# Layer 1's feed-forward with seven products of sums of half blocks in place of eight

## The chip, the core and the metric

The kernel runs on one core of one Trainium2 chip. The metric is the device time of one execution in microseconds, and less is better. The core's engines work from queues of their own: TensorE (PE in the profile, with its weight loads as PEld) multiplies, VectorE (DVE), ScalarE (ACT) and GpSimd (POOL) do the elementwise work, and SyncE (SP) issues nearly all of the transfers (DMA) between SBUF and DRAM. Products are accumulated in eight PSUM banks.

## The reference, cut to what matters

A two-layer transformer trunk works on 1024 tokens of width 1024, with 256 context tokens in layer 0. Each layer has a mixer and a gated feed-forward with 2816 hidden features. Layer 1's feed-forward and the final norm are what the change touches:

```
def _swiglu(x, w_in, w_out):
    a, b = jnp.split(x @ w_in, 2, axis=-1)
    return (jax.nn.silu(a) * b) @ w_out

x = x + mx[5] * _swiglu(_modulate(_rms(x, norm_ffn[layer]), mx[3], mx[4]),
                        ffn_in[layer], ffn_out[layer])
...
return _rms(x, norm_final)
```

Everything is float32. The kernel gets near float32 with reduced-precision products: each operand is split into a high part and a low part, and a product is three matmuls (high by high, low by high, high by low; `mm3`, L104 to 107).

## The kernel before, in words

**Layout.** Features lie on the 128 partitions. The 1024 tokens are two chunks of 512 (`c` = 0 and 1). A tile of activations is [128, 8, 512]: eight blocks of 128 features. `act` holds four buffers of 16 KB per partition (tag a16) and two of 8 KB (a8).

**A pair of parts.** `split` (L94 to 102) makes them: ACT copies the source to the high part (L96), DVE (L100) or POOL (L102) subtracts it for the low part. `load_w` (L240 to 252) loads a weight block [128, 1024] on SP's queue into `raw` and splits it. It takes pools pwA and pwB in turn.

**Layer 1's mixer output.** `MixerOut.block` (L786 to 795) multiplies one of eight weight blocks with one chunk, adds the result to the residual `x[c]` on DVE (L793) and adds its square to a running sum (`Rms.add`, ACT L187/L190 and POOL L194). Chunk 0 is finished inside the retention stage, chunk 1 in the `sweep`. `Rms.finish` (L196 to 213) sums over partitions with PE (L203), takes the power -1/2 with Ln and Exp on ACT (L208, L209), corrects it (L210, L211) and leaves the scale vector `rstd` (L213). `Rms.apply` (L215 to 224) multiplies (L218, DVE) and splits (L223 ACT, L224 DVE). The normalization of a chunk is deferred: it is put into the queues behind the first product of the next work (`run_deferred`).

**The feed-forward, `ffn` (L815 to 857).** The hidden features are 22 blocks (`j`, NJ). For each block and chunk, `f_in` makes two products over eight k-blocks (24 matmuls each), ACT takes Silu of the first (L827), DVE multiplies by the second (L828), and the result is split into `hh` and `hl`. `f_out` multiplies it with eight column blocks of the output weights (24 matmuls) and adds each to `x[c]` with the gate (L845, DVE). `f_out` runs one step behind `f_in`. The hidden result stays in SBUF, and every output product is added to the residual at once.

**The end.** In `final1` (L1402) chunk 1's last output runs in two halves of 256 tokens, and `done1` defers each part's final norm and stores (L1395, L1397).

**What sets the order.** The program text is handed to a planner, which gives each engine its queue: among the instructions whose inputs and buffers are there it takes the one that comes first in the text. On the chip each queue is then worked off in that order. Memory pools are a stack: a pool opened after others were closed lies on their bytes, its tags one after the other in the order of first use. With `reuse_waits="tile"` a new tile waits for the users of the earlier tiles on its own bytes, and for nothing else. Before layer 1's feed-forward the stack, above `act`, is pwA (20 KB: raw 4, wh 8, wl 8), `x[0]` (16), the small tiles t2j (20), `x[1]` (16) and pwB3 (24).

Of the kernel before, what the change touches and what calls it, by code (L numbers as in the profile page):

```python
# [39 lines left out]
def dit(ctx, tc, A, out):  # L40
# [50 lines left out]
    def col(name, n):  # L91
        return cols[:, CO[name] : CO[name] + n]
# [10 lines left out]

    def mm3(ps, wh, wl, xh, xl, first, last):  # L104
        te.matmul(ps, wh, xh, start=first, stop=False)  # L105
        te.matmul(ps, wl, xh, start=False, stop=False)  # L106
        te.matmul(ps, wh, xl, start=False, stop=last)  # L107
# [24 lines left out]
    def ada_block(l, typ, b, whichs):  # L132
        blk = typ * KB + b
        if (l, typ) not in parts:
            parts[l, typ] = T(cst, [P, KB, 2, 2], f"pt_{l}{typ}")
        for h in range(2):
            w = T(cst, [P, 512], "adaw", bufs=2)
            with tc.issue_after(mark[0]):
                sy.dma_start(w, A["ada"][l, blk, h])
            for which in whichs:  # L140
                jk = T(cst, [P, 1024], "junk", BF16)
# [132 lines left out]

# [1 line left out]
    ocd = [T(dram, [P, 8, n], f"oc{c}") for c, (_, n) in enumerate(CH)]  # L276
# [182 lines left out]
    def v_post(gi):  # L459
# [5 lines left out]
        for i, tb in enumerate(tbs):  # L465
# [37 lines left out]

# [1 line left out]
    sD = es()  # L505
# [93 lines left out]

# [1 line left out]
    sE = es()  # L601
# [147 lines left out]
    sA.close()  # L749
# [1 line left out]
    psE = es()  # L751
# [213 lines left out]
    sL2.close()  # L965
# [1 line left out]
    SC = 64 ** -0.5  # L967
# [26 lines left out]

# [1 line left out]
    psI = es()  # L996
# [155 lines left out]
    sG.close()  # L1152
# [1 line left out]
    psJ = es()  # L1154
# [209 lines left out]
    sJ.close()  # L1364
# [24 lines left out]
    def done1(c, s):
        def later(r=rm1[c]):  # L1390
            n = r.n
            r.finish()
            for b in range(KB):
                y = x[c][:, b, s]
                ve.scalar_tensor_tensor(y, y, col("nfin", 8)[:, b : b + 1], r.r[:, :n], op0=ALU.mult, op1=ALU.mult)  # L1395
                if b % 2:
                    sy.dma_start(out[c, :, b - 1 : b + 1, s], x[c][:, b - 1 : b + 1, s])  # L1397

        run_deferred()
        deferred.append(later)  # L1400

    def final1(f_in, f_out, prev):  # L1402
        f_in(NJ - 1, 0)
        prev()
        f_in(NJ - 1, 1)
        f_out(NJ - 1, 0)
        f_out(NJ - 1, 1, slice(0, 256))
# [117 lines left out]
```

## Time and profile before

| | |
|---|---|
| median of 3 runs | 2883.57 us (2882.09 to 2884.86) |
| span of the profiled execution | 2883.5 us |
| mean granted TensorE clock | 0.982 |
| q1, SP's transfers | 210.89 MB |
| layer 1's mixer output and feed-forward | from about 2080 us to the end |

The profile is one execution. Its page gives busy times and shares of each engine, the span in 40 slices, the chain of work that ended last, and groups of instructions with their count, busy time, mean ns of one, and the idle time ahead of them with what ended it. A view of the trace answers for a stretch of time: a row of the timeline is start, duration, engine, line, operation, output<-inputs and shape; a row of the windows is, for a stretch, the busy time and count of each engine, the granted clock, the share of the transfer engines and GB/s. Matmuls overlap, so the duration of one (0.39 us) is longer than the distance between two.

### The profile page before, as it was taken

How to read it: one execution, taken by the hardware profiler on the slowest of the kernel's cores; microseconds unless marked ns; L12 is line 12 of the kernel's file. 1: busy time of each engine (PE TensorE's matmuls, PEld its weight loads, DVE VectorE, ACT ScalarE, POOL GpSimd, SP SyncE). 2: the span in 40 equal slices, each digit the busy share in tenths (PEclk: the TensorE clock that was granted, in tenths of full speed). 3: DMA queues.
4: the chain of work that ended last, by engine and by line, in shares of the span. 5: the costliest groups of instructions: out<-in, count | busy, mean ns of one | idle time of the engine just before them, and what ended most of it. 6: DMA issues, size and time to landing. Idle time of an engine off the chain costs nothing.

```text
span 2883.5 us, 35705 instructions
## 1 busy us (share of the span) xinstructions
PE 2740.1 (95%) x13928; PEld 2308.7 (80%) x13928; DVE 1716.4 (60%) x3174; ACT 931.5 (32%) x1579; POOL 769.1 (27%) x476
## 2 busy tenths in 40 slices
PE   6998899998999999999999899898899999999997
PEld 4876788787888888888888787786688888888886
DVE  8779776457665555564445546887654444444446
ACT  5425455544111111111113434676551111111113
POOL 2132122352111212121213146443342112211222
PEclk8999999999999999999999999999999999999998
DMA  6343010441222222221111122124321111111111
GB/s 234 106 149 105 25 37 27 169 131 63 70 70 74 81 66 73 66 88 45 44 37 62 70 92 78 63 63 135 123 74 59 44 44 51 52 51 44 44 44 59
DMA packets 90649, 217.37 MB, mean 75 GB/s; under 512 B 8816, under 2 KB 24944, under 8 KB 89456
## 3 DMA queue, kind: packets, MB, share of 16 engines
q1 hardware_dynamic: 88800, 210.89, 22.5%
q8 instruction: 110, 1.80, 0.3%
q0 software_dynamic: 432, 2.62, 0.2%
q10 hardware_dynamic: 1248, 1.57, 0.1%
q14 instruction: 59, 0.48, 0.1%
HBM read 193.03 MB, written 22.02 MB: 75 GB/s over the span
## 4 chain that ended last, share of the span: by engine, by line
PE 71%; DVE 14%; DMA 5%; ACT 4%; issue 3%; POOL 2%; SPq 0%; POOLq 0%; DVEq 0%; ACTq 0%
PE ps L105 22%; PE ps L107 22%; PE ps L106 22%; DVE junk L142 3%; DMA adaw<-in_ada_dram 3%; PE ps L686 1%; DVE t2k L218 1%; DVE sm L1083 1%; DVE st L666 1%; ACT P L669 1%; DVE spt L100 1%; PE ps L183 1%; POOL wl L102 1%; ACT wh L96 1%; PE ps L203 1%
## 5 line engine op out<-in xcount | busy, mean ns | idle before, releaser
L105 PE MATMUL ps<-a,wh 128*128 128x512 f32 (+1 forms) x2488 | 929.2, 374 | 15.7 <-ACT a L223 7.1
L106 PE MATMUL ps<-a,wl 128*128 128x512 f32 (+1 forms) x2488 | 921.7, 371 | 10.1 <-DVE wl L100 7.6
L107 PE MATMUL ps<-a,wh 128*128 128x512 f32 (+1 forms) x2488 | 919.9, 370 | 2.5 <-DVE a L224 1.8
L102 POOL TENSOR_TENSOR wl<-raw,wh 128x1024 fp32r<-128x1024 f32 x181 | 445.8, 2466 | 1400.0 <-ACT wh L96 1399.7
L105 PEld LDWEIGHTS ps<-a,wh 128*128 128x128 f32 x2488 | 474.1, 191 | 101.1 <-ACT a L223 9.1
L106 PEld LDWEIGHTS ps<-a,wl 128*128 128x128 f32 x2488 | 473.6, 190 | 94.4 <-DVE wl L100 10.4
L107 PEld LDWEIGHTS ps<-a,wh 128*128 128x128 f32 x2488 | 473.4, 190 | 82.9 <-DVE a L224 3.6
L828 DVE TENSOR_TENSOR t2k<-t2k,ps 128x512 f32<-128x512 f32 (+1 forms) x110 | 69.6, 633 | 624.6 <-PE ps L107 624.6
L105 PE MATMUL ps<-hh,wh 128*128 128x512 f32 (+1 forms) x888 | 327.2, 368 | 4.1 <-ACT hh L96 2.5
L107 PE MATMUL ps<-hl,wh 128*128 128x512 f32 (+1 forms) x888 | 325.8, 367 | 1.1 <-DVE hl L100 1.1
L106 PE MATMUL ps<-hh,wl 128*128 128x512 f32 (+1 forms) x888 | 326.3, 367 | 0.0
L845 DVE SCALAR_TENSOR_TENSOR x<-ps,md,x 128x512 f32<-128x512 f32 (+1 forms) x528 | 312.3, 653 | 4.6 <-PE ps L107 4.6
L96 ACT ACTIVATE wh<-raw 128x1024 fp32r<-128x1024 f32 x193 | 203.9, 1058 | 276.8 <-PE ps L107 157.9
L827 ACT ACTIVATE t2k<-ps 128x512 f32<-128x512 f32 (+1 forms) x110 | 61.1, 555 | 672.0 <-PE ps L107 671.9
L845 DVE SCALAR_TENSOR_TENSOR xk<-ps,md,xk 128x512 f32<-128x512 f32 (+1 forms) x360 | 241.0, 730 | 3.2 <-PE ps L107 3.2
L142 DVE CUSTOM_DVE_ANT_0 junk<-adaw,cond_x 128x512 bf16<-128x512 f32 x160 | 132.2, 826 | 172.4 <-DMA adaw<-in_ada_dram 170.3
L96 ACT ACTIVATE hh<-t2k 128x512 fp32r<-128x512 f32 (+1 forms) x110 | 64.2, 584 | 410.7 <-DVE t2k L828 410.7
L105 PEld LDWEIGHTS ps<-hh,wh 128*128 128x128 f32 x888 | 168.2, 189 | 33.1 <-ACT hh L96 2.9
L107 PEld LDWEIGHTS ps<-hl,wh 128*128 128x128 f32 x888 | 167.9, 189 | 29.0 <-DVE hl L100 1.5
L106 PEld LDWEIGHTS ps<-hh,wl 128*128 128x128 f32 x888 | 168.1, 189 | 27.4 <-issue 0.2
L100 DVE TENSOR_TENSOR hl<-t2k,hh 128x512 fp32r<-128x512 f32 (+1 forms) x110 | 135.0, 1228 | 2.9 <-ACT hh L96 1.8
L194 POOL TENSOR_TENSOR acc<-t2k,acc 128x512 f32<-128x512 f32 (+1 forms) x71 | 84.5, 1192 | 134.9 <-ACT t2k L190 132.7
(277 smaller groups left out, 3565.8 us busy)
## 6 DMA issues: line engine op xcount, KB each, us to landing
raw<-in_w_fi_dram SPq DMA_DIRECT2D x88, 512.0 KB, 3.7
adaw<-in_ada_dram SPq DMA_DIRECT2D x160, 256.0 KB, 2.7
raw<-in_w_fo_dram SPq DMA_DIRECT2D x44, 512.0 KB, 3.7
raw<-in_w_cd_dram SPq DMA_DIRECT2D x26, 512.0 KB, 3.7
raw<-in_w_cdo_dram SPq DMA_DIRECT2D x16, 512.0 KB, 3.8
raw<-in_w_abo_dram SPq DMA_DIRECT2D x14, 512.0 KB, 3.8
a<-in_ada_dram SPq DMA_DIRECT2D x12, 512.0 KB, 9.7
t2k<-oc SPq DMA_DIRECT2D x24, 256.0 KB, 3.1
```

Of the source, the lines that this page charges most:

```text
L96: ac.activation(hi, src, AF.Identity)
L100: ve.tensor_tensor(lo, src, f32(hi), op=ALU.subtract)
L102: po.tensor_tensor(lo, src, f32(hi), op=ALU.subtract)
L105: te.matmul(ps, wh, xh, start=first, stop=False)
L106: te.matmul(ps, wl, xh, start=False, stop=False)
L107: te.matmul(ps, wh, xl, start=False, stop=last)
L142: ve.tensor_tensor_reduce(jk[:, :512], w, cond[which][:, h * 512 : h * 512 + 512], op0=ALU.mult, op1=ALU.add, scale=1.0, scalar=0.0, accum ...
L183: te.matmul(self.ps, ones, sq[:, :n], start=self.count == 1, stop=self.count == self.total)
L194: po.tensor_tensor(self.acc[:, :n], sq[:, :n], self.acc[:, :n], op=ALU.add)
L827: ac.activation(s[:, :n], pa, AF.Silu)
L828: ve.tensor_tensor(s[:, :n], s[:, :n], pb, op=ALU.mult)
L845: ve.scalar_tensor_tensor(xm, ps[:, s], mod(l, which(c), GATE_F, m), xm, op0=ALU.mult, op1=ALU.add)
```

## The change

With A the weights and B the activations, a product of 2 x 2 half blocks is made from seven products instead of eight (Winograd's form of Strassen's method). For the input half, A is the block's two halves a and b by two halves of the features, and B is two halves of the features by two chunks. The sums of B (T1 to T4) are made once; the sums of A (S1 to S4, `comb_w`) for every block.

- `Seven.first` (chunk 0 alone) makes B11 and B21; `Seven.second` makes B22 and T1 to T4 from both chunks, in place in `x[0]` and `x[1]`. The residual is therefore stored to DRAM before (`spill`, `xr`) and read back later.
- `fin_front(j)` makes the two products A11 B11 and A12 B21 of a block with weights of its own (`fr`, `w1`), up to LEAD = 3 blocks ahead; `fin_back(j)` loads the block's weights again, makes the sums, and the other five products, with three read-outs between products that share a bank.
- The hidden result of two blocks gives the seven B operands of the output half (`hid_out`), which go to DRAM (`hd`); the sums of the output weights go to DRAM too (`wo_out`, `sd`).
- The output half (`fout`) runs one of the seven products at a time over all of the hidden features, in 6 steps each; `load_b` reads both operands of a step from DRAM and splits them, two steps ahead in the text. Two groups of four banks hold the sums, and x is updated only at the end of each product. Chunk 0's final norm comes before the seventh product.
- Pools: pA, opened when the pools of the mixer and x are closed, holds fr (8 KB), w1 (16), acc (6), g0 (8), w8 (48) and t2k (16), in this order; pT, with T1 and T4, lies at the other end of the memory. To make room, the tiles of the condition (cond_x, adaw, junk) move to a pool at that end that is closed after layer 0, POOL's transfer scratch is cut to 1024 bytes, and the three stores of `oc` go from POOL's queue to SP's.

```diff
-        po.dma_start(ocd[c][:, 4:8], u[c])
+        sy.dma_start(ocd[c][:, 4:8], u[c])
...
+        def first(self, r):
+            self.scaled(0, r)
+            self.plain("B11", 0, 0)
+            self.plain("B21", 0, 1)
+
+        def second(self, r):
+            x0, x1 = self.x
+            self.scaled(1, r)
+            lo4, hi4 = slice(0, 4), slice(4, 8)
+            ve.tensor_tensor(x0[:, lo4], x1[:, lo4], x0[:, lo4], op=ALU.subtract)
+            for k in range(4):
+                ve.scalar_tensor_tensor(x1[:, k], x1[:, k + 4], self.d[k], x1[:, k], op0=ALU.add, op1=ALU.subtract)
+            self.plain("B22", 1, 1)
+            for k in range(4):
+                y = x1[:, k + 4]
+                ve.scalar_tensor_tensor(y, y, self.sh[k + 4], x0[:, k], op0=ALU.add, op1=ALU.subtract)
+            self.comb("T2", x1[:, hi4], "dve")
+            self.comb("T3", x1[:, lo4], "pool")
+            for k in range(4):
+                y = x0[:, k + 4]
+                ve.scalar_tensor_tensor(y, y, self.sh[k + 4], x1[:, k + 4], op0=ALU.add, op1=ALU.subtract)
+            self.comb("T1", x0[:, lo4], "dve")
+            self.comb("T4", x0[:, hi4], "pool")
+
+    def comb_w(raw, e):
+
+        e.tensor_tensor(raw[:, 3], raw[:, 2], raw[:, 3], op=ALU.add)
+        e.tensor_tensor(raw[:, 2], raw[:, 0], raw[:, 2], op=ALU.subtract)
+        e.tensor_tensor(raw[:, 0], raw[:, 3], raw[:, 0], op=ALU.subtract)
+        e.tensor_tensor(raw[:, 1], raw[:, 1], raw[:, 0], op=ALU.subtract)
...
+    def fin_front(l, j):
+        raw = T(pA, [P, 2, 512], "fr", F32, 2)
+        sy.dma_start(raw.rearrange("p a n -> p (a n)"), A["w_fi"][l, j, 0])
+        w = T(pA, [P, 2, 2, 512], "w1", F32R, 2)
+        w = w[:, 0], w[:, 1]
+        cut(w[0], w[1], raw, "pool")
+        X = T(pp, [P, 512], "ps")
+        mm4(X, w, 0, "B11", True, True)
+        s1 = t2k("acc")
+        ac.activation(s1, X, AF.Identity)
+        Y = T(pp, [P, 512], "ps")
+        mm4(Y, w, 1, "B21", True, True)
+        g = T(pA, [P, 512], "g0", F32, 4)
+        ve.tensor_tensor(g, Y, s1, op=ALU.add)
+        ac.activation(g, g, AF.Silu)
+        pre[j] = X, g
+
+    def fin_back(l, j):
+        X, g0 = pre.pop(j)
+        raw = w8([P, 4, 512])
+        for h in range(2):
+            sy.dma_start(raw[:, 2 * h : 2 * h + 2].rearrange("p a n -> p (a n)"), A["w_fi"][l, j, h])
+        w2 = w8([P, 2, 1, 512], F32R)
+        cut(w2[:, 0], w2[:, 1], raw[:, 3:4], "dve")
+        comb_w(raw, ve)
+        w3 = w8([P, 2, 2, 512], F32R)
+        cut(w3[:, 0], w3[:, 1], raw[:, 0:2], "pool")
+        w4 = w8([P, 2, 2, 512], F32R)
+        cut(w4[:, 0], w4[:, 1], raw[:, 2:4], "dve")
+        w2, w3, w4 = ((w[:, 0], w[:, 1]) for w in (w2, w3, w4))
+        mm4(X, w3, 0, "T2", False, True)
+        u1 = t2k("acc")
+        ac.activation(u1, X, AF.Identity)
+        Z = T(pp, [P, 512], "ps")
+        mm4(Z, w4, 0, "T3", True, True)
+        m7 = t2k("acc")
+        ac.activation(m7, Z, AF.Identity)
+        mm4(X, w4, 1, "T1", False, True)
+        h1 = t2k()
+        ve.tensor_tensor(h1, X, m7, op=ALU.add)
+        mm4(Z, w2, 0, "T4", False, True)
+        h0 = t2k()
+        ve.tensor_tensor(h0, Z, u1, op=ALU.add)
+        mm4(X, w3, 1, "B22", False, True)
+        g1 = T(pA, [P, 512], "g0", F32, 4)
+        ac.activation(g1, X, AF.Silu)
+        ve.tensor_tensor(h0, h0, g0, op=ALU.mult)
+        ve.tensor_tensor(h1, h1, g1, op=ALU.mult)
+        hid[j] = h0, h1
...
+    for j in range(LEAD):
+        fin_front(1, j)
+    for j in range(NJ):
+        fin_back(1, j)
+        if j + LEAD < NJ:
+            fin_front(1, j + LEAD)
+        if j % 2:
+            hid_out(j // 2)
+        else:
+            wo_out(1, j // 2)
...
+    def load_b(l, i, b):
...
+        raw = w8([P, 2, 2, 512])
+        if a in SI:
+            sy.dma_start(raw[:, 0, :n], sd[b][:, SI[a], :n])
+        else:
...
+            for q in range(n):
+                sy.dma_start(raw[:, 0, q], A["w_fo"][l, j0 + 2 * q, :, hs])
+        sy.dma_start(raw[:, 1, :n], hd[b][:, HI[h], :n])
+        k = steps.index((i, b))
+        t = act_tile(0, [P, 2, 2, 2, 512]) if k % 4 < 2 else T(pT, [P, 2, 2, 2, 512], "tx", F32R, 2)
+        ac.activation(t[:, 0, :, :n], raw[:, :, :n], AF.Identity)
+        po.tensor_tensor(t[:, 1, 0, :n], raw[:, 0, :n], f32(t[:, 0, 0, :n]), op=ALU.subtract)
+        ve.tensor_tensor(t[:, 1, 1, :n], raw[:, 1, :n], f32(t[:, 0, 1, :n]), op=ALU.subtract)
+        ready[i, b] = t
...
+    def fout(l):
+        bank = {}
+        halves = [slice(0, 256), slice(256, 512)]
+        for k in range(2):
+            load_b(l, *steps[k])
+        for c in range(2):
+            x[c] = act_tile(0, [P, 8, 512], F32)
+            sy.dma_start(x[c], xr[c])
+        for k, (i, b) in enumerate(steps):
+            a, h, bk, start, c, m0 = PROD[i]
+            if k + 2 < len(steps):
+                load_b(l, *steps[k + 2])
...
```

More of the change, by code (lines that the diff above doesn't have):

```diff
@@ new lines, in comb_w, with spill, t_alloc @@
+    def comb_w(raw, e):
[3 more added lines that the diff above has]
+        e.tensor_tensor(raw[:, 1], raw[:, 1], raw[:, 0], op=ALU.subtract)
+    rmx = {0: mo.rm[0]}
+    def spill(c, m):
+        sy.dma_start(xr[c][:, m], x[c][:, m])
+    for m in range(KB):
+        spill(0, m)
+    def t_alloc(name):
+        if name in ("B11", "B21", "B22", "T2"):
+            t = act_tile(0, [P, 2, 4, 512])
+        elif name == "T3":
+            return act_tile(2, [P, 4, 512]), act_tile(2, [P, 4, 512])
+        else:
+            t = T(pT, [P, 2, 4, 512], "tx", F32R, 2)
+        return t[:, 0], t[:, 1]
@@ new lines, in dit, with first @@
+    sv = Seven(1, x, t_alloc)
+    def first():
+        rmx[0].finish()
+        sv.first(rmx[0])
+    deferred.append(first)
+    for m in range(KB):
+        mo.block(m, 1, acts)
+        spill(1, m)
+    mo.rm[1].finish()
+    sv.second(mo.rm[1])
+    sF.close()
+    sL.close()
+    pA = sA = es()
+    pA = pool(sA, "pA")
+    t2p[0] = pA
+    t2n.update(t2k=8, acc=3, rstd=2)
+    NP = NJ // 2
+    hd = [T(dram, [P, 7, 2, 512], f"hd{b}") for b in range(-(-NP // 2))]
+    sd = [T(dram, [P, 4, 2, 512], f"sd{b}") for b in range(-(-NP // 2))]
@@ new lines, in dit, with w8, mm4 @@
+    HI = {n: i for i, n in enumerate(("B11", "B21", "T2", "T3", "T1", "T4", "B22"))}
+    SI = {n: i for i, n in enumerate(("S2", "S4", "S3", "S1"))}
+    hid, pre = {}, {}
+    def w8(shape, dt=F32):
+        return T(pA, shape, "w8", dt, 6)
+    def mm4(ps, w, wi, t, first, last):
+        for k in range(4):
+            ks = slice(k * P, k * P + P)
+            mm3(ps, w[0][:, wi, ks], w[1][:, wi, ks], sv.t[t][0][:, k], sv.t[t][1][:, k], first and k == 0, last and k == 3, not first)
+    def fin_front(l, j):
[14 more added lines that the diff above has]
+        pre[j] = X, g
@@ new lines, in hid_out @@
+    def hid_out(p):
+        (b11, b12), (b21, b22) = hid.pop(2 * p), hid.pop(2 * p + 1)
+        t1, t2, t4 = t2k(), t2k(), t2k()
+        ve.tensor_tensor(t1, b12, b11, op=ALU.subtract)
+        ve.tensor_tensor(b12, b22, b12, op=ALU.subtract)
+        ve.tensor_tensor(t2, b22, t1, op=ALU.subtract)
+        ve.tensor_tensor(t4, b21, t2, op=ALU.subtract)
+        for n, t in (("B11", b11), ("B21", b21), ("B22", b22), ("T1", t1), ("T2", t2), ("T3", b12), ("T4", t4)):
+            sy.dma_start(hd[p // 2][:, HI[n], p % 2], t)
@@ new lines, in dit @@
+    x = [None, None]
+    PROD = [("A11", "B11", 0, True, 0, 0), ("A12", "B21", 1, True, 0, 0), ("S2", "T2", 0, False, 0, 4), ("S3", "T3", 1, True, 1, 4),
+            ("S1", "T1", 0, False, 1, 4), ("A22", "T4", 1, False, 0, 4), ("S4", "B22", 0, False, 1, 0)]
+    steps = [(i, b) for i in range(7) for b in range(len(hd))]
+    ready = {}
+    def load_b(l, i, b):
+        a, h = PROD[i][:2]
+        n = min(2, NP - 2 * b)
+        raw = w8([P, 2, 2, 512])
+        if a in SI:
+            sy.dma_start(raw[:, 0, :n], sd[b][:, SI[a], :n])
+        else:
+            hs = slice(0, 512) if a[1] == "1" else slice(512, 1024)
+            j0 = 4 * b + (a[2] == "2")
+            for q in range(n):
[7 more added lines that the diff above has]
+        ready[i, b] = t
```

140 lines of the change are left out of this document (99 added, 41 removed).

## The prediction

> **What bounds the kernel now.** I read the page first (engine shares, slices, chain), then the windows of layer 1's feed-forward, then its groups by form, then single rows at its two ends.
>
> ```profile
> span 2883.5 us, 35705 instructions
> PE 2740.1 (95%) x13928; PEld 2308.7 (80%) x13928; DVE 1716.4 (60%) x3174; ACT 931.5 (32%) x1579; POOL 769.1 (27%) x476
> PE   6998899998999999999999899898899999999997
> PE 71%; DVE 14%; DMA 5%; ACT 4%; issue 3%; POOL 2%; SPq 0%; POOLq 0%; DVEq 0%; ACTq 0%
> ```
> ```profile
> 2200.00:2840.00 640.00, 640.00 (x2825) 530.14 (x2824) 286.77 (x392) 104.31 (x135) 136.39 (x57) 1.00 0.14 45
> ```
>
> The span is 2883.5 us, and the median of the three runs is 2883.57, so the profile stands for the runs. PE carries 71% of the chain. The windows row says more: in the 640 us inside layer 1's feed-forward (columns: PE, PEld, DVE, ACT, POOL busy with counts, granted clock, DMA share, GB/s) PE is never idle and the clock is 1.00. So every matmul taken out here shortens the kernel by its spacing, 640/2825 = 0.2265 us, as long as PE stays fed. DVE is 45% busy, POOL 21%, the transfers 14%: there is room, but the change spends it.
>
> **The matmuls.** The feed-forward has 22 hidden blocks. Now each has 96 input products (two halves, two chunks, 8 k-blocks, 3 each) and 48 output products, 3168 in all. After it, seven block products of 12 give 84 per hidden block, and the output half has 7 x 11 x 4 x 3 = 924: 1848 + 924 = 2772. 396 fewer at 0.2265 are **-89.7 us**.
>
> **Prices of the added work.**
>
> ```profile
> L102 POOL TENSOR_TENSOR wl<-raw,wh 128x1024 fp32r<-128x1024 f32 x57 | 136.4, 2393 | 483.8 <-ACT wh L96 483.8
> L96 ACT ACTIVATE wh<-raw 128x1024 fp32r<-128x1024 f32 x57 | 60.4, 1059 | 152.1 <-PE ps L107 112.7 <-issue 39.4
> L828 DVE TENSOR_TENSOR t2k<-t2k,ps 128x512 f32<-128x512 f32 x39 | 26.8, 688 | 348.9 <-PE ps L107 348.9
> L96 ACT ACTIVATE hh<-t2k 128x512 fp32r<-128x512 f32 x39 | 24.4, 625 | 112.7 <-DVE t2k L828 112.7
> L827 ACT ACTIVATE t2k<-ps 128x512 f32<-128x512 f32 x39 | 23.3, 598 | 267.2 <-PE ps L107 267.2
> ```
> ```profile
> L100 DVE TENSOR_TENSOR wl<-raw,wh 128x1024 fp32r<-128x1024 f32 x3 | 3.7, 1226 | 7.4 <-ACT wh L96 7.4
> ```
> ```profile
> L194 POOL TENSOR_TENSOR acc<-t2k,acc 128x512 f32<-128x512 f32 x47 | 64.6, 1376 | 110.6 <-ACT t2k L190 109.2
> ```
> ```profile
> 2226.75 2.40 POOL L102 TENSOR_TENSOR wl<-raw,wh 128x1024 fp32r<-128x1024 f32 x1 [2.62 <-ACT wh L96]
> ```
> ```profile
> 2225.63 0.69 DVE L828 TENSOR_TENSOR t2k<-t2k,ps 128x512 f32<-128x512 f32 x1 [9.63 <-PE ps L107]
> 2226.24 1.43 DVE L845 SCALAR_TENSOR_TENSOR xk<-ps,md,xk 128x512 f32<-128x512 f32 x2
> 2227.59 2.11 DVE L100 TENSOR_TENSOR hl<-t2k,hh 128x512 fp32r<-128x512 f32 x1
> ```
> ```profile
> 2308.62 0.69 DVE L100 TENSOR_TENSOR hl<-t2k,hh 128x512 fp32r<-128x512 f32 x1
> ```
>
> The rows of L100 with hl are the ones to remember. The same DVE subtraction, both operands in SBUF, takes 0.69 us alone and 2.11 when it meets POOL's operation of 2226.75 to 2229.15: it ends 0.55 after POOL does, so it waited it out. Work of the two on SBUF pairs is therefore one queue here. A DVE operation with a PSUM operand (L828, 688) doesn't wait.
>
> The Trainium skill (SBUF — State Buffer, Who interferes with whom) has this as a rule: a DVE instruction with two SBUF inputs and a GpSimd instruction that reads SBUF exclude each other for a whole instruction. By that rule each such pair costs its sum; the trace agrees (2.11 against 0.69).
>
> **One hidden block, input half.** PE needs 84 x 0.2265 = 19.0 us.
> - POOL: low parts of w1 and w3, 2 x 2.39, and half of the four sums of the output weights, 2 x 1.38: 7.5.
> - DVE on SBUF pairs: low part of w2 0.69, four weight sums 2.76, low part of w4 1.23, two products with the gate 1.38, half of the four hidden sums 1.38: 7.4. DVE from PSUM: three sums, 2.1.
> - ACT: three high parts of 1024 at 1.06, one of 512 at 0.63, three copies at 0.60, two Silu at 0.6: 6.8.
>
> With every exclusion paid, DVE needs 7.4 + 7.5 + 2.1 = 17.0 of 19.0; with none 9.5. Nobody exceeds PE, so throughput holds. The latency is tighter. X, Z and X again are accumulated in two banks, and each is read out between its products; one product of cover is 12 x 0.2265 = 2.72. ACT's copies (0.60, behind at most one 1.06) fit. DVE's h1 must run between T1 and B22: if one POOL operation and one 1024-wide cut stand ahead, 2.39 + 1.23 + 0.69 = 4.3, 1.6 too late. So the wait per block lies between 0 (the queue happens to be clear) and 1.6. I take 0.7, nearer the middle since DVE is near 90% taken: **+15 us** (0 to 35). The weights for the next block are costed at nothing: six buffers of 8 KB hold the next block's raw, w2 and w3 while this one's multiply. The price without that cover is the second rival. The planner already orders work by readiness and not by the program text: at 2226.24 two sums of L845, which the text has after L100, run before it.
>
> **The entry.** Now the second chunk's normalization hides behind 48 matmuls. After the change it is followed by sums of half chunks, and only B11 and B21 are ready before.
>
> ```profile
> 2137.15 0.75 DVE L793 SCALAR_TENSOR_TENSOR xk<-ps,md,xk 128x512 f32<-128x512 f32 x1 [4.69 <-PE ps L107]
> ...
> 2146.34 0.69 DVE L213 SCALAR_TENSOR_TENSOR rstd<-t2k,t2k 128x512 f32<-128x512 f32 x1
> 2147.14 2.08 DVE L218 SCALAR_TENSOR_TENSOR t2k<-xk,md,rstd 128x512 f32<-128x512 f32 x3
> ```
>
> From the last sum of the mixer to the scale vector: 9.9 us. Then DVE in `second`: 8 scalings at 0.69, one 2048-wide difference (0.69 and 1.23 extended: 2.3), 4 differences, 4 low parts of B22, 4 for T2, its low part 2 x 1.23, 4 for T4, the low part of T1 2 x 1.23: 24 operations at 0.69, 2.3 and 4.9, 23.8 us. POOL has T3 and T4, 4 x 2.39 = 9.6, which DVE can't overlap. The end lies at 9.9 + 23.8 = 33.7 to 43.3.
>
> What can PE do meanwhile? Three fronts would be 72 matmuls, 16.3 us. But pool pA lies on the bytes of the pools just closed. By the order of its tags its second w1 buffer begins at 16 KB and ends at 24, and the old pools have pwA on the first 20 KB and x0 on the next 16: that buffer, the acc buffers (24 to 30) and three of g0 lie on x0, which T1 and T4 read last. So only the first front, 24 matmuls or 5.4 us, runs ahead; the second waits for x0 and then for its split, 1.06 + 2.39 = 3.5. Bounds: 43.3 + 3.5 - 5.4 = 41; and, if the first w1 buffer were used again and no exclusion paid, 33.7 + 3.5 - 16.3 = 21. I take **+36**, near the upper end, by the 2.11 row. After it PE starts slowly:
>
> ```profile
> 679.12 0.80 PE L105 MATMUL ps<-a,wh 128*128 128x512 f32 x1 [5.23 <-ACT a L223]
> ...
> 680.14 0.63 PE L105 MATMUL ps<-a,wh 128*128 128x512 f32 x1
> 680.57 0.63 PE L106 MATMUL ps<-a,wl 128*128 128x512 f32 x1
> ```
> ```profile
> 684.41 0.63 PE L105 MATMUL ps<-a,wh 128*128 128x512 f32 x1
> 684.83 0.45 PE L106 MATMUL ps<-a,wl 128*128 128x512 f32 x1
> 685.12 0.40 PE L107 MATMUL ps<-a,wh 128*128 128x512 f32 x1
> ```
>
> After 5.23 us idle the spacing is 0.43 from 680.14 to 684.83 and 0.29 after: some 13 matmuls at 0.2 extra, **+3**. The Trainium skill (TensorE: Matmul & The Clock Gate, What's actually happening) says the clock falls to half after an idle window of about 3.4 us; by that rule the gap costs the same 3, and the rows agree. The 16 spills of 256 KB (x to DRAM) hide in the mixer's sweep and the 9.9 us.
>
> **The second half.** A step is 24 matmuls, 5.4 us; its preparation is ACT 2048 wide (0.43 more per 512: 1.9), POOL 2.39 and DVE 1.23, and the loads are 1 MB.
>
> ```profile
> q1 hardware_dynamic: 88800, 210.89, 22.5%
> raw<-in_w_fi_dram SPq DMA_DIRECT2D x88, 512.0 KB, 3.7
> xd<-x SPq DMA_DIRECT2D x2, 2048.0 KB, 6.3
> ```
>
> 1.05 MB per 5.44 us is 193 GB/s. The queue moved 210.89 MB in 22.5% of the span (649 us of all engines): 325 GB/s when busy. The load is 59%, and no engine has more than 3.6 of 5.4 us, so the steps cost nothing extra while four operand and six raw buffers run ahead. Were only one step ahead, 3.7 + 1.9 + 2.4 + 1.2 = 9.2 would show, 3.8 per step. At the start the two 2 MB reloads of x share the queue: 12.6 + 3.7 + 4.3 until the third step is ready against two steps, 10.9, at most 9.7. Between 0 and that: **+5**.
>
> **The end.** Now chunk 0's final scaling stands on DVE behind the last matmul; after the change it runs under the seventh product.
>
> ```profile
> 2861.05 0.28 PE L107 MATMUL ps<-hl,wh 128*128 128x256 f32 x1
> ```
> ```profile
> 2864.04 6.67 DVE L1395 SCALAR_TENSOR_TENSOR xk<-xk,cols,rstd 128x512 f32<-128x512 f32 x8
> ...
> 2873.19 6.42 DVE L1395 SCALAR_TENSOR_TENSOR xk<-xk,cols,rstd 128x256 f32<-128x256 f32 x16
> ```
>
> Of those 6.67 us some stay covered by the halves' own sums of squares: 0 to -7, I take **-4**. The moved stores of `oc` (POOL's queue to SP's) and the moved condition tiles: 0; behind the stores on SP wait weight loads, issued ahead.
>
> Sum: 2883.5 - 89.7 + 15 + 36 + 3 + 5 - 4 = **2849**.
>
> **The rivals.**
> 1. *The entry is covered.* If PE gets all three fronts and T1's cut goes early, the gap is under 21 and the waits few: 2849 - 20 - 15 = 2814. For it: PE loses nothing at this place now. Against: the byte count above.
> 2. *The input products wait for their weights* (slower). On DVE the sums for block j+1 stand behind the last reads of block j: 0.69 for g, 1.38 hidden sums, 0.69 + 2.76, then ACT 1.06 and POOL 2.39, 9.0 us against 24 matmuls or 5.4; 3.6 per block, up to 11 with POOL's 7.5 in between. 22 x 4.3 instead of 15 is +80: 2929. It decides from 2.2 us per block, (2883.5 - 2834)/22. For it: DVE at 17 of 19 us. Against: one block of look-ahead in the buffers.
> 3. *The second half is bound by transfers.* At 150 GB/s the 40.4 MB (7 x 11 x 512 KB) take 269 us against 209: +60, 2909. It decides below about 166 GB/s, where the cost is the 34.5 us left. Against: 325 GB/s while busy.
> 4. *The clock falls in many short waits.* The Trainium skill (TensorE: Matmul & The Clock Gate, A second HAM failure mode) tells of that where PE cycles through banks. In this trace:
>
> ```profile
> 2000.00:2040.00 40.00, 32.22 (x194) 23.70 (x193) 34.85 (x79) 27.14 (x40) 18.17 (x19) 0.91 0.13 40
> ```
>
> PE busy 32 of 40 us, clock 0.91. On 419 us of input products that is +41: 2890. Against: waits of under 2 us in a stage at 90%.
> That the matmuls don't fall by 396 I hold for excluded: the loops are counted out.
>
> **How the numbers follow.** Chances: forecast 0.55 (its own range 2815 to 2885), rival 1 0.13, rival 2 0.17, rival 3 0.09, rival 4 0.06. A measurement of this kernel tells about 0.2% (6 us) from no change. Faster: 0.53 + 0.13 + 0.02 + 0.01 = 0.69. Same: 0.02 + 0.01 + 0.02 + 0.02 = 0.07. Slower: 0.16 + 0.05 + 0.03 = 0.24. The range 2806 to 2912 leaves out the worse part of rival 2 (0.11), the best of rival 1 (0.04) and the forecast's own ends (0.04).
>
> **What would show it.** Right: 2772 products in the feed-forward; one PE gap of 25 to 40 us at the entry that ends on w1 and x0's last cuts; short gaps of PE before B22 that end on DVE's sum; the second half solid; DVE subtractions of 2 us and more. Wrong: PE waiting in every block for POOL's or DVE's low weight parts (rival 2), for loads in the second half (3), a clock under 0.95 in the input half (4), or an entry gap under 20 (1).

## The result and the profile after

The kernel after the change takes 2918.93 us in the median of four runs (2916.43 to 2920.64), the kernel before 2882.83 (2878.53 to 2884.86). The ratio is 1.0123 with an interval of 1.0111 to 1.0136: slower by 1.2%, where 2849 had been forecast, with a range that ended at 2912. The page of the kernel after, as far as it answers to what was shown of before:

```profile
span 2917.9 us, 35510 instructions
PE 2685.9 (92%) x13520; PEld 2251.5 (77%) x13520; DVE 1750.8 (60%) x3100; ACT 1034.9 (35%) x1669; POOL 912.2 (31%) x541
PE   6988899998999999999999998998849998988998
PEclk9999999999999999999999999999979999999999
PE 57%; DVE 16%; DMA 8%; issue 6%; POOL 6%; ACT 5%; SPq 1%; DVEq 0%; POOLq 0%; ACTq 0%
```

The matmuls went as counted: 408 rows fewer (13928 to 13520), of which 396 are the products and 12 come from fewer blocks cut in halves at the end. But PE's share of the chain fell from 71% to 57%, and transfers, waiting to issue and POOL, 10% of it before, now hold 20%. The windows of the kernel after (columns as in the prediction) show where: a stretch of the input half, and 20 us late in the second half.

```profile
2200.00:2640.00 440.00, 401.66 (x1677) 324.96 (x1676) 220.98 (x260) 129.71 (x178) 144.49 (x79) 0.96 0.46 156
2860.00:2880.00 20.00, 16.89 (x55) 11.10 (x54) 11.19 (x13) 10.89 (x11) 8.11 (x4) 0.83 0.02 9
```

In the first row 1677 matmuls at 0.2265 are 379.8 us, and the stretch lasts 440: 60 us lost. Reckoned from the start of one matmul to the start of the next, 40 of them are eleven gaps of more than 1 us, 16.5 are matmuls that run slowly behind most of these gaps (the granted clock is 0.96 in the mean), and some 4 are spread over the rest.

**One gap, row by row.** The timeline of the kernel after around 2340 us, all engines, in order of time:

```profile
2324.46 1.20 SPq L1569 DMA_DIRECT2D w<-in_w_fo_dram  x2
2326.22 4.19 SPq L1564 DMA_DIRECT2D hd<-t2k  x6
2330.50 1.28 POOL L1449 TENSOR_TENSOR w<-w 128x512 f32<-128x512 f32 x1 [7.19 <-DMA w<-in_w_fo_dram]
...
2334.61 1.29 POOL L1452 TENSOR_TENSOR w<-w 128x512 f32<-128x512 f32 x1
2335.93 0.57 SPq L1571 DMA_DIRECT2D sd<-w  x1
2336.55 1.68 SPq L1527 DMA_DIRECT2D w<-in_w_fi_dram  x2
2342.40 0.40 PE L111 MATMUL ps<-tx,w 128*128 128x512 f32 x1
2343.96 0.63 ACT L1389 ACTIVATE w<-w 128x512 fp32r<-128x512 f32 x1 [6.12 <-DMA w<-in_w_fi_dram]
2344.68 0.69 DVE L1391 TENSOR_TENSOR w<-w,w 128x512 fp32r<-128x512 f32 x1 [12.12 <-ACT w L1389]
2345.29 0.68 DVE L1545 TENSOR_TENSOR t2k<-ps,acc 128x512 f32<-128x512 f32 x1
2346.03 0.50 PE L109 MATMUL ps<-a,w 128*128 128x512 f32 x1 [3.23 <-DVE t2k L1545]
```

Read it from the bottom. PE stands from about 2342.6 until h1 (line 1545) has run on DVE. DVE had been idle for 12.12 us; it runs h1 only behind the low part of the next block's w2 (line 1391), because that instruction stands ahead in DVE's queue. That one waits for ACT's high part, which waits for the next block's raw weights. They were issued at 2336.55 although SP had issued nothing between 2330.4 and 2335.93: the store of the output-weight sums (line 1571) stood at the head of SP's queue until POOL ended the last of its four sums (2334.61 + 1.29 = 2335.90). In ten of the eleven rounds up to the second half the next block's loads went out within 0.4 us behind this store, so they had been ready. Two blocks share one such store, and one gap.

The waits of the kernel after, 2190 to 2640 us (engine, line, waited for: us in total, times, longest; SPq is SP's queue):

```profile
SPq L1571 <- POOL w L1452: 53.0, 10, 5.8
POOL w L1449 <- DMA w<-in_w_fo_dram: 75.2, 10, 11.4
ACT w L1389 <- DMA w<-in_w_fi_dram: 67.5, 12, 7.5
PEld ps L109 <- DVE t2k L1545: 38.8, 10, 5.1
PE ps L109 <- DVE t2k L1545: 34.4, 10, 4.6
```

**What a gap of 4 to 5 us costs.** The rows of PE that follow the gap at 2297.6 to 2302.5 in the kernel after:

```profile
2302.51 0.61 PE L109 MATMUL ps<-a,w 128*128 128x512 f32 x1 [4.49 <-DVE t2k L1545]
2302.92 0.63 PE L110 MATMUL ps<-a,w 128*128 128x512 f32 x1
...
2306.49 0.39 PE L110 MATMUL ps<-a,w 128*128 128x512 f32 x1
2306.72 0.40 PE L111 MATMUL ps<-a,w 128*128 128x512 f32 x1
```

The spacing is 0.43 until about 2306 and 0.23 after, 1.7 us extra. Measured from start to start, the gaps from 3.5 to 5.0 us in this stretch are followed by 1.6 to 3.0 us of this kind, all but one (3.66); the gaps of 1.28 and 2.38 us are not. So a wait of 4.7 really costs some 6.4. The Trainium skill (TensorE: Matmul & The Clock Gate, HAM oscillation — how this bites in real kernels) tells of just such a loop, where a wait longer than a window of about 3.4 us comes back in every round and each time puts the clock to half. By that rule gaps above the window pay and shorter ones don't. The rows of this stretch agree in the main, but the length of a gap alone doesn't decide: in experiment 2 below a gap of 2.77 us was followed by a granted clock of 0.51 (2211.36 to 2214.70) and one of 3.81 us by 1.00 (2230.30 to 2236.00).

**Where the 34.4 us between the two spans (2883.5 and 2917.9) come from**, forecast beside measured. The stages are bounded by rows of the timeline: the last sum of the mixer on DVE (line 797 after), PE at work again (2183.08), the first matmul of the second half (2676.4), the last product (2905.0).

| part | forecast | measured |
|---|---|---|
| until the mixer's last sum (2137.15, then 2141.54) | 0 | +4.4 |
| matmuls | -89.7 | -89.7 |
| entry (36 for the gap, 3 for the slow clock behind it; the latter, 1.8, is measured in the next row) | +39 | +41.5 |
| input half, beyond 1848 x 0.2265 = 418.6 | +15 | +74.7 |
| second half, beyond 924 x 0.2265 = 209.3 | +5 | +19.3 |
| end, from the last product | -4 | -9.4 |
| what before had in its feed-forward beyond 3168 x 0.2265 | 0 | -6.3 |

The measured column adds up to 34.5. The first row can't be put down to the change: in the twelve kernels below nothing ahead of that point is altered (but in 4, 8, 9 and 11, which put loads of the fronts there, 4 their matmuls too), and in their profiled executions the last sum came anywhere between 2130.8 and 2142.1. The medians below therefore carry some us of that scatter, and I compare **stages**: A from the mixer's last sum to the first matmul of the second half, and B from there to the end of the span. Stages scatter too. B lies between 240.3 and 242.1 in the nine kernels of the table that leave it alone; A read 534.9 in the kernel after and 539.7 in kernel 6, which doesn't touch it.

### The profile page after: what moved, and what is told of

It is laid out like the page before. It is cut to its first block, busy times and chain, and to the rows that moved or that the text cites. A ratio compares the mean times of both kernels' runs of the same rounds, so it can differ in the third digit from the quotient of the medians.

```text
span 2917.9 us, 35510 instructions
## 1 busy us (share of the span) xinstructions
PE 2685.9 (92%) x13520; PEld 2251.5 (77%) x13520; DVE 1750.8 (60%) x3100; ACT 1034.9 (35%) x1669; POOL 912.2 (31%) x541
## 4 chain that ended last, share of the span: by engine, by line
PE 57%; DVE 16%; DMA 8%; issue 6%; POOL 6%; ACT 5%; SPq 1%; DVEq 0%; POOLq 0%; ACTq 0%
PE ps L109 17%; PE ps L110 17%; PE ps L111 17%; DMA w<-in_w_fi_dram 3%; DVE junk L146 2%; DMA adaw<-in_ada_dram 2%; POOL tx L1607 1%; POOL a L1607 1%; DMA w<-in_w_fo_dram 1%; DVE t2k L222 1%; PE ps L690 1%; DVE sm L1088 1%; ACT w L1389 1%; DVE w L1391 1%; DVE st L670 1%
## 5 line engine op out<-in xcount | busy, mean ns | idle before, releaser
L109 PE MATMUL ps<-a,wh 128*128 128x512 f32 (+1 forms) x1784 | 656.2, 368 | 19.9 <-ACT a L227 7.6
L110 PE MATMUL ps<-a,wl 128*128 128x512 f32 (+1 forms) x1784 | 649.3, 364 | 8.2 <-DVE wl L104 7.0
L111 PE MATMUL ps<-a,wh 128*128 128x512 f32 (+1 forms) x1784 | 647.9, 364 | 2.3 <-DVE a L228 1.7
L106 POOL TENSOR_TENSOR wl<-raw,wh 128x1024 fp32r<-128x1024 f32 x115 | 283.8, 2471 | 870.0 <-ACT wh L100 869.8
L109 PEld LDWEIGHTS ps<-a,wh 128*128 128x128 f32 x1784 | 342.3, 192 | 78.3 <-ACT a L227 9.4
L110 PEld LDWEIGHTS ps<-a,wl 128*128 128x128 f32 x1784 | 341.8, 192 | 64.5 <-DVE wl L104 9.9
L111 PEld LDWEIGHTS ps<-a,wh 128*128 128x128 f32 x1784 | 341.5, 191 | 55.2 <-DVE a L228 3.3
L109 PE MATMUL ps<-a,w 128*128 128x512 f32 x440 | 180.9, 412 | 73.8 <-ACT w L1389 39.4
L109 PE MATMUL ps<-hh,wh 128*128 128x512 f32 (+1 forms) x528 | 189.3, 358 | 3.1 <-ACT hh L100 2.1
L111 PE MATMUL ps<-hl,wh 128*128 128x512 f32 (+1 forms) x528 | 188.5, 358 | 1.0 <-DVE hl L104 1.0
L110 PE MATMUL ps<-hh,wl 128*128 128x512 f32 (+1 forms) x528 | 188.8, 358 | 0.0
L110 PE MATMUL ps<-a,w 128*128 128x512 f32 x440 | 178.5, 406 | 6.5 <-POOL w L1391 6.5
L111 PE MATMUL ps<-a,w 128*128 128x512 f32 x440 | 177.7, 404 | 0.0
L109 PEld LDWEIGHTS ps<-a,w 128*128 128x128 f32 x440 | 87.2, 198 | 98.4 <-ACT w L1389 41.1
```

Source lines behind the costliest of these rows:

```text
L106: po.tensor_tensor(lo, src, f32(hi), op=ALU.subtract)
L109: te.matmul(ps, wh, xh, start=first, stop=False, skip_group_check=more)
L110: te.matmul(ps, wl, xh, start=False, stop=False, skip_group_check=more)
L111: te.matmul(ps, wh, xl, start=False, stop=last, skip_group_check=more)
```

## The experiments

Each is the kernel after with the edit shown. The theory: SP's queue stands at the store of the sums, and through the next block's weights and DVE's queue PE stands too. Against it: the buffers, DVE's load, or POOL's and DVE's hold on each other.

| kernel | median us | against before (interval) | A | B |
|---|---|---|---|---|
| after | 2918.93 | 1.0123 (1.0111 to 1.0136) | 534.9 | 241.5 |
| 1 store on ACT | 2875.97 | 0.9979 (0.9970 to 0.9989) | 493.5 | 241.9 |
| 2 w2's low part on POOL | 2918.81 | 1.0120 (1.0103 to 1.0136) | 538.7 | 241.2 |
| 3 no sums | 2858.48 | 0.9915 (0.9900 to 0.9930) | 478.0 | 241.4 |
| 4 fronts in the mixer's end | 2925.62 | 1.0153 (1.0137 to 1.0169) | 547.8 | 240.8 |
| 5 store after the next loads | 2860.19 | 0.9919 (0.9903 to 0.9936) | 480.0 | 242.1 |
| 6 late norm of chunk 0 | 2914.96 | 1.0110 (1.0093 to 1.0127) | 539.7 | 235.3 |
| 7 edits 5 and 6 | 2856.90 | 0.9902 (0.9887 to 0.9917) | 480.0 | 235.9 |
| 8 fronts behind the ones | 2910.48 | 1.0093 (1.0078 to 1.0108) | 531.2 | 241.1 |
| 9 edits 5, 6 and 8 | 2849.30 | 0.9884 (0.9866 to 0.9901) | 472.6 | 235.6 |
| 10 T3, T4 cut on DVE | 2912.46 | 1.0116 (1.0098 to 1.0134) | 532.9 | 241.5 |
| 11 edits 5, 6, 8 and 10 | 2840.59 | 0.9866 (0.9850 to 0.9883) | 468.1 | 235.3 |
| 12 sums twice | 2966.28 | 1.0296 (1.0281 to 1.0312) | 586.7 | 240.3 |

**1. The store on ACT's queue.**

```diff
-        sy.dma_start(sd[p // 2][:, :, p % 2], raw)
+        ac.dma_start(sd[p // 2][:, :, p % 2], raw)
```

> The store of the output-weight sums (line 1571) is issued from ACT's queue instead of SP's; the sums stay on POOL. Theory A (order in SP's queue: the store stands there until POOL's sums end at about 2336 us, the next block's raw weight loads are behind it, their cut on DVE is late and stands ahead of h1): the one PE gap of 3.6 to 5.0 us per two blocks, about 51 us in all, goes for the greater part, and with it most of some 20 us of slow clock; 2918.9 falls by 30 to 65 us, to 2854 to 2889. Theory B (the loads are late because their buffer comes free late, or because DVE has too much to do between T1 and B22): the gaps stay, 2914 to 2924. Theory C (the store only moves the block from SP to ACT: ACT then stands at the store while POOL sums, and its cuts and copies wait): gaps of the same size that end on ACT, 2910 to 2935.

Stage A fell by 41 us, so the store's place matters: theory A. But C holds in part too. ACT's timeline in this kernel:

```profile
2329.35 0.52 ACTq L1571 DMA_DIRECT2D sd<-w  x1
2329.91 0.63 ACT L1520 ACTIVATE g<-g 128x512 f32<-128x512 f32 x1 [5.99 <-DMA w<-in_w_fi_dram]
```

ACT now stands 5.99 us at the store, and copies that PE needs (line 1538) come late: PE waits for them 10 times between 2190 and 2600, up to 2.2 us. (The row names a transfer; what had just gone ahead of it on ACT is the store.)

**2. w2's low part on POOL.**

```diff
-        cut(w2[:, 0], w2[:, 1], raw[:, 3:4], "dve")
+        cut(w2[:, 0], w2[:, 1], raw[:, 3:4], "pool")
```

> The low part of w2 is cut on POOL instead of DVE; SP's queue is as it was, so the raw loads land as late as before. Theory A (h1 waits behind w2's low part in DVE's queue): the sums of the same block's weights (line 1449 on DVE) come next in that queue and wait for the same loads, so h1 is only free if they stand behind it; the gap of 3.6 to 5.0 us per two blocks changes by less than 2 us each, 2900 to 2925 (faster only if the sums stand behind h1). Theory B (DVE's load: too much work between T1 and B22): 0.4 us of DVE's work a block goes, the gaps shrink by that, 2905 to 2917.

No change (2918.81). Taking the one instruction ahead of h1 off DVE isn't enough, and 0.7 us less of DVE's work a block brings nothing that shows. The gaps are still there and end elsewhere: PE's weight loads now wait 28.4 us (9 times between 2190 and 2640) for ACT's copy of line 1542, ahead of which ACT has high parts of the next block's weight sums (2320.38 ahead of 2321.34 in one round). The late weights reach PE by another queue.

**3. Without the sums** (the stored S operands are the raw weights, as the expectation says).

```diff
-        comb_w(raw, po)
```

> The four sums of the output weights are left out in the first half (the stored S operands are the raw weights, so the second half computes with other operands of the same size); their store stays on SP and waits only for its loads. Theory A in the form that POOL's sums are what the store waits for: SP goes on about 5 us earlier per two blocks and the gaps vanish, 2855 to 2890. Theory A in the form that the loads of the output weights (landing late, 11 us of wait at line 1449) hold the store: the gap shrinks by part of the 5.4 us that the sums take, 2890 to 2910. Theory D (POOL's sums share a port with DVE and make DVE slow there): DVE's operations in the stretch become shorter by a third, the gaps halve, 2885 to 2905.

Stage A fell by 57 us, the first of the three forms. The window of this kernel shows an input half as solid as the one before:

```profile
2200.00:2560.00 360.00, 358.55 (x1567) 293.38 (x1566) 206.48 (x240) 120.27 (x165) 86.48 (x36) 1.00 0.51 178
```

This can't yet tell the store's wait from the work of POOL itself (theory D). The next one can.

**5. The store behind the next loads.** POOL sums as ever, SP stores; only the place of the store in the text differs.

```diff
         comb_w(raw, po)
-        sy.dma_start(sd[p // 2][:, :, p % 2], raw)
+        held.append((p, raw))
...
             fin_front(1, j + LEAD)
+        if held:
+            p, raw = held.pop()
+            sy.dma_start(sd[p // 2][:, :, p % 2], raw)
```

> POOL sums the output weights as in the kernel after, and SP issues the store of the sums, but the store stands in the text behind the loads of the next block's weights. Theory A (order in SP's queue alone): as good as leaving the sums out, since nothing then waits for the sums; the gaps of 3.6 to 5.0 us go, the input half falls from 493 us to 425 to 440, and the time to 2852 to 2875. Theory D (it is POOL's work itself that slows DVE or fills the time, so leaving it out helped and moving its store does not): 2895 to 2920.

Stage A fell by 55 us, within 2 of leaving the sums out. The windows and the timeline of this kernel:

```profile
2200.00:2580.00 380.00, 375.48 (x1632) 306.88 (x1631) 202.23 (x254) 125.87 (x172) 143.34 (x76) 1.00 0.50 172
```
```profile
2353.28 1.36 POOL L1449 TENSOR_TENSOR w<-w 128x512 f32<-128x512 f32 x1 [10.23 <-DMA w<-in_w_fo_dram]
2355.65 0.86 SPq L1527 DMA_DIRECT2D w<-in_w_fi_dram  x2
2357.80 1.29 POOL L1452 TENSOR_TENSOR w<-w 128x512 f32<-128x512 f32 x1
2359.12 0.57 SPq L1584 DMA_DIRECT2D sd<-w  x1
```

POOL waits as long for its loads as before (10.23 us here) and the store still waits for POOL, to 2359.12. But the block's raw weights went out at 2355.65, ahead of it, while POOL was summing. The store's wait no longer holds up weights that PE needs: PE is busy 375.5 of 380 us at a mean clock of 1.00, and 3.9 of the 4.5 us missing are one gap at the start, which ends at 2225.11. POOL's work and the number of buffers are as they were, so theory D is out, and too few buffers as well.

**12. The sums twice** (the second half then computes with other operands).

```diff
         comb_w(raw, po)
+        comb_w(raw, po)
```

> POOL does the four sums of the output weights twice (the second time on the results of the first, so the second half computes with other operands), the store on SP waits for both; nothing else differs from the kernel after. Theory A (whatever POOL takes is time that SP's queue stands, and after it PE): each of the ten gaps of 3.6 to 5.0 us grows by the 5.4 us of four sums, 10 x 5.4 = 54 us, to 2960 to 2985. Theory B (buffers or DVE's load set the gaps): under 15 us more.

Stage A grew by 51.8 us, 54 forecast. POOL's eight sums and SP's store in this kernel, and PE's wait (2240 to 2640):

```profile
2390.45 1.29 POOL L1449 TENSOR_TENSOR w<-w 128x512 f32<-128x512 f32 x1 [7.33 <-DMA w<-in_w_fo_dram]
...
2399.93 1.29 POOL L1452 TENSOR_TENSOR w<-w 128x512 f32<-128x512 f32 x1
2401.25 0.57 SPq L1572 DMA_DIRECT2D sd<-w  x1
2401.86 0.63 SPq L1527 DMA_DIRECT2D w<-in_w_fi_dram  x1
```
```profile
PEld ps L109 <- DVE t2k L1545: 66.3, 8, 8.9
```

The gaps, 4.2 us in the mean in the kernel after (the same view), are 8.3 here: 4.1 us more each and not 5.4, so some 1.3 us of what POOL takes were covered. (The planner also put one of the block's two raw loads ahead of the store here; the other, at 2401.86, still stands behind it.) PE's idle time between 2200 us and the second half grew by 42 us, from 48 to 90, and most of the other 10 is the slow clock behind the gaps.

**6. Chunk 0's norm later.**

```diff
-                if lastb and i == 5:
-                    done1(0, slice(0, 512), rm1[0])
+                if i == 6 and b == 2:
+                    done1(0, slice(0, 512), rm1[0])
```

> The final norm of chunk 0 (its four matmuls with the ones, its scaling and stores) stands in the text behind the third step of product 7 instead of behind product 6; the rest is the kernel after. Theory: PE stands about 10 us at those matmuls because the squares and POOL's sums that they read end late; 16 us of product 7 now stand ahead of them, so the stall goes: 2918.9 falls by 7 to 11 us, to 2908 to 2912. Rival (chunk 0's scaling and stores now fall into the tail and lengthen it by as much): 2914 to 2922.

The rows of the kernel after that this removes, POOL and PE:

```profile
2862.22 2.40 POOL L1607 TENSOR_TENSOR tx<-w,tx 128x1024 fp32r<-128x1024 f32 x1 [2.01 <-ACT tx L1606]
2864.59 2.24 POOL L198 TENSOR_TENSOR acc<-t2k,acc 128x512 f32<-128x512 f32 x1
2866.88 2.07 PE L207 MATMUL ps<-acc,ones 128*128 128x512 f32 x2 [3.11 <-POOL acc L198]
```

PE, four matmuls into product 7, stands at the ones because POOL adds chunk 0's last squares behind an operand cut (2862.22). With the norm later, stage B is 6.2 us shorter and the gap is gone. That is somewhat less than the 7 to 11 expected, and it shows in the median as 4; stage A read 4.8 longer in the profiled execution.

**7. Edits 5 and 6.**

> The store of the sums behind the next loads and the late norm of chunk 0 together. If the two causes stand side by side, the gains add: 2843 to 2866. If the first stall hides part of the second (PE comes earlier to the norm, whose squares wait for the same transfers), 2 to 8 us less is gained.

2856.90, in the range; stages A and B each repeat the single gains (480.0 and 235.9). They add.

**4. The fronts' products in the mixer's end.** The three fronts' weights are loaded and cut in the mixer's weight buffers, and their products stand ahead of chunk 1's mean square in the text; `fin_front` then takes X and Y from there.

```diff
+    for j in range(LEAD):
+        w = [t.rearrange("p (a n) -> p a n", a=2) for t in load_w(A["w_fi"][1, j, 0])]
...
+        ahead[j] = X, Y
     mo.rm[1].finish()
     sv.second(mo.rm[1])
```

> The two products each of the first three fronts are put ahead of chunk 1's preparation in the text, with their weights cut in the buffers of the mixer's weights; the rest is the kernel after. Theory (the entry's gap of about 41 us on PE is queue order: the fronts' weight cuts stand behind those of T4 on ACT and POOL although their operands B11 and B21 have long been there): 48 matmuls a front, 3 x 2 x 48 = 288 matmuls at 0.2265 us = 65 us are ready to run in the gap; the gap closes but for what chunk 1's chain leaves, 2918.9 falls by 15 to 42 us, to 2877 to 2904. Rival (the cuts of the fronts delay chunk 1's chain by as much as PE gains, or the operands B11 and B21 are late themselves): 2912 to 2925.

A miss: slower by 7. The forecast's 288 matmuls were a miscount (3 x 2 x 12 = 72, 16 us), and the edit put them in the wrong place: PE does them ahead of the ones of chunk 1's mean square, which ended at 2150.8 where the last sum was at 2133.7 (2145.6 and 2141.5 in the kernel after). It also moved the first half's buffers, and the first block's raw weights were issued only at 2185.89 instead of 2149.36. Number 8, with the old addresses, issues them at 2143.54.

**8. The fronts behind the ones.** As 4, but with `mo.rm[1].finish()` ahead of the loop, and with fr, w1 and acc still taken first, so that the buffers keep their addresses.

> The first three fronts' products stand behind the matmuls of chunk 1's mean square and ahead of chunk 1's preparation, and the buffers of the first half keep the addresses that they have in the kernel after. A front is 2 products of 12 matmuls, so the three are 72 matmuls, 16 us at 0.2265 (the 288 matmuls and 65 us of the earlier expectation were a miscount). Theory (the gap at the entry is partly queue order): PE does these 16 us while chunk 1 is prepared and the gap shrinks by 8 to 16 us: 2903 to 2911. Rival (the three cuts on ACT and POOL hold up chunk 1's chain by what PE gains, or the first block's own weights come late): 2914 to 2924.

Stage A fell by 3.7 us only (the median by 8.4), less than A scatters. PE and DVE in this kernel:

```profile
2157.30 0.39 PE L111 MATMUL ps<-a,wh 128*128 128x512 f32 x1
2188.68 0.80 PE L109 MATMUL ps<-a,w 128*128 128x512 f32 x1 [30.99 <-ACT w L1389]
```
```profile
2168.04 6.64 DVE L1391 TENSOR_TENSOR tx<-xk,tx 128x1024 fp32r<-128x1024 f32 x2
2180.63 0.69 DVE L1449 TENSOR_TENSOR w<-w 128x512 f32<-128x512 f32 x1
2181.36 2.71 DVE L1450 TENSOR_TENSOR w<-w 128x512 f32<-128x512 f32 x1
```

PE does the fronts while chunk 1 is prepared and then stands 31 us more, for block 0's own weights: their sums on DVE come behind the whole of chunk 1's chain. Both theories were half right; what ended late next is the rival's second clause.

**10. T3 and T4 cut on DVE.**

```diff
-            self.comb("T3", x1[:, lo4], "pool")
+            self.comb("T3", x1[:, lo4], "dve")
...
-            self.comb("T4", x0[:, hi4], "pool")
+            self.comb("T4", x0[:, hi4], "dve")
```

> The low parts of T3 and T4 are cut on DVE instead of POOL; the rest is the kernel after. In the profile after, two cuts of T3 on POOL take 10.88 us while DVE works, where one alone takes 2.4, and DVE's operations beside them 2.8 in place of 0.75 and 3.4 in place of 1.2. Theory (DVE and POOL hold each other up there): DVE takes on four cuts of 1.2 (4.9 us) and gets back about 4 to 5 us, its chain ends about as before, and POOL is free to cut the front's weights 5 us earlier: PE restarts 2 to 6 us earlier, 2911 to 2917. Rival (DVE's chain only gets longer): 2919 to 2925.

POOL in the kernel after, then DVE and PE in this one:

```profile
2159.99 10.88 POOL L1391 TENSOR_TENSOR a<-xk,a 128x1024 fp32r<-128x1024 f32 x2 [15.58 <-ACT a L1389]
```
```profile
2159.26 4.62 DVE L1391 TENSOR_TENSOR a<-xk,a 128x1024 fp32r<-128x1024 f32 x4
2166.45 4.62 DVE L1391 TENSOR_TENSOR tx<-xk,tx 128x1024 fp32r<-128x1024 f32 x4
2173.34 0.79 PE L110 MATMUL ps<-a,w 128*128 128x512 f32 x1 [3.49 <-POOL w L1391]
```

The two cuts of T3 that took POOL 10.88 us are two of the four (T2's and T3's) that DVE does in 4.62. PE restarts 38.2 us after the mixer's last sum (2135.1) instead of 41.5; in the eight kernels that leave the entry alone it is 41.2 to 42.5, so a gain of 3 to 4 us is clear, at the lower end of what was expected. Stage A's 2.0 are within its scatter, and the median's 6.5 hold scatter of the mixer.

**9 and 11. The mends together.**

> The store behind the next loads, the late norm of chunk 0, and the fronts behind the matmuls of the mean square. By their own stages the three gained 55 us (input half), 6 us (second half) and 3.7 us (from the mixer's last sum to the end of the input half): if they add, about 4 us less than the first two together, 2850 to 2856; if the fronts ahead bring nothing once the input half runs without gaps, 2855 to 2859.

> The three mends and the cuts of T3 and T4 on DVE together: 2 to 6 us under the three mends alone if the cuts' place matters at the entry, else the same within 2 us.

Freed of the gaps, stage A shows both edits: 480.0 in kernel 7, 472.6 with the fronts, 468.1 with the cuts as well, so they gain 7.4 and 4.5 us and the mends add. The medians are 2849.30, 0.7 under the first range, and 2840.59; the 8.7 between them hold scatter of the mixer (its last sum came at 2142.1 and at 2135.6). Against before the last is 0.9866 (0.9850 to 0.9883), faster by 1.3%, and PE has no gap between 2200 and 2560 us:

```profile
2200.00:2560.00 360.00, 360.00 (x1577) 295.57 (x1576) 192.33 (x246) 123.62 (x169) 137.44 (x73) 1.00 0.51 177
```

## Why the prediction was wrong, point by point

**The bound and the matmuls** were right: PE was the limit, 396 products went, and where PE is fed a matmul takes close to the 0.2265 taken (360 us for 1577 in experiment 11 are 0.228).

**The step that failed** is the input half: +15 us (bounds 0 to 35), measured +74.7. Two sentences of it fell. "DVE's h1 must run between T1 and B22" named the right wait, but its price was made only from what DVE and POOL execute (4.3 us against 2.72 of cover). What stood ahead of h1 was an instruction that itself waited, for weights that hadn't been sent. And "the weights for the next block are costed at nothing: six buffers ... hold the next block's raw, w2 and w3" counted room and not the order of issue. The change adds a store on SP that waits for POOL, between loads that PE needs. The prediction asked what is queued behind the stores of `oc`, and not behind that of line 1571, at which SP stood 53.0 us in ten waits. Experiment 5 shows it: the same work with only that order changed takes 55 us off. It leaves some 20 us over 418.6, within the bounds, but they aren't the forecast's 0.7 us in every block: in the 380 us shown PE is idle for 4.5 us, 3.9 of them in one gap, and half of the 20 lies at the two ends of the input half. The exclusion of DVE and POOL, for which the +15 stood, cost PE next to nothing there.

**The rivals.** The second (weights come late, 2929) has the right size, +80 in the input half, and the right late thing, but not the mechanism: it put the delay into DVE's own work, and experiment 5 leaves all of that work there. That its size fits is luck. The fourth (many short waits lower the clock, +41) was a part: 16.5 of the 60 us lost between 2200 and 2640 are slow matmuls. They go with the gaps (clock 1.00 in experiment 5).

**The entry** was near in its size, 36 (bounds 21 to 41) against 41.5 and 3 against 1.8 for the slow clock, and wrong in one part: the first front was to run ahead, and only two of its matmuls started before the gap's end, at 2176. ACT cut the front's weights at 2174.93, directly behind T4's cut, POOL at 2180.68 behind its own. That is queue order, and experiment 8 shows that undoing it alone gains little, since block 0's weight sums are late next. That the cuts on POOL and DVE's work hold each other up (10.88 for two cuts) was forecast from the 2.11 row and is borne out by experiment 10, small as it is.

**The second half** was +5 for its start, measured +19.3. PE's rows in the kernel after tell the parts apart. The start costs 6.6 us: two gaps, which end on the operands of the third step as forecast, and a granted clock of 0.50 from 2695.28 to 2702.11.

```profile
2694.86 1.74 PE L109 MATMUL ps<-tx 128*128 128x512 f32 x4 [1.92 <-ACT tx L1606]
2698.34 1.22 PE L110 MATMUL ps<-tx 128*128 128x512 f32 x2 [1.75 <-POOL tx L1607]
```

From 2863.39 to 2873.14 chunk 0's matmuls with the ones cost 9.3 us, stall and slow clock included; the stall was not foreseen, and experiment 6 takes 6.2 us off. The ones of chunk 1's first half, from 2902.03, cost 2.2, and the last 1 is spread. (The kernel before has eight ones of chunk 0 too, from 2854.8; they are part of the table's last row.) That transfers don't bind it (rival 3) was right: from 2702.5 to 2862 PE is never idle, at a clock of 1.00.

**The end**: -9.4 against -4, with 0 to -7 as bounds. 13.0 us are left behind the last product instead of 22.4. Some of this only changed its row: the ones of chunk 1's first half came behind the last product before (from 2861.2) and come ahead of it now (the 2.2 above). The other 7 fit the whole 6.67 us of chunk 0's scaling, which was then uncovered; no experiment tests this.

Of the 69 us between forecast and measurement 60 are thus the input half; of the others the largest is the second half with 14, and some of it is made up by the end and by the table's last row. With the store's order mended alone the kernel stands at 2860.2, and with the two smaller edits of experiment 9 at 2849.3. That this is the forecast's 2849 is luck, since these edits aren't part of what was forecast.

## What to carry to other kernels

For each transfer that a change adds, write down what the issuing instruction waits for and which loads come after it in the same queue: a store that waits for a slow engine belongs behind the next loads; here its wait then cost nearly nothing (stage A 480.0, against 478.0 without the sums). Follow the wait through every queue to PE, since here one transfer in SP's queue reached PE by way of ACT's and DVE's; buffers for a block ahead help only if the loads that fill them can be issued. Price a wait that returns in every round with the slow clock behind it: the gaps of 4 to 5 us here cost about 2 us more than their length.

## What the runs showed of the hardware

- DVE and POOL hold each other up in both directions: two cuts on POOL that take 2.4 us each alone took 10.88 beside a busy DVE, and a sum on DVE took 2.71 instead of 0.69 beside POOL (2181.36 in experiment 8). The Trainium skill (SBUF — State Buffer, Who interferes with whom) has a rule that an instruction of the one blocks the other for its whole length; the rows agree. What I had not expected is how long POOL is held beside a DVE that goes from one such instruction to the next: the first of the two cuts took 8.13 us (2159.99 to 2168.12), while DVE began nine instructions of its own; the second took 2.78.
- An instruction that waits in SP's queue holds back loads that are ready: SP issued nothing for 5.5 us (2330.4 to 2335.93), and the next block's loads went out 0.05 us behind the store. In experiment 5, where they stand ahead of it, they go out while POOL still sums.
- In the kernel after, gaps of PE up to 2.4 us in the input half (from start to start, 2200 to 2640) left the clock as it was; of those from 3.5 to 5.0 us, all but one were followed by 7 to 14 slow matmuls, mostly at 0.43 us. This is no sharp threshold: two gaps of 2.31 and 2.38 us close together at the start of the second half were followed by a clock of 0.50, and so was one of 2.62 us in experiment 1 (2231.5 to 2234.9), while one of 3.81 us in experiment 2 was not.
